# Pairs of delta heads in one inverse, unnormed keys and queries, and smaller first blocks, in a hybrid decoder layer on one core

## The chip, the cores and the metric

The kernel runs on one core of one Trainium2 chip. The metric is device time in microseconds (us). Before the change three runs gave a median of 906.72 us (906.41 to 909.12).

## The reference

One decoder layer is computed in fp32 for a prompt of 512 tokens and for 32 sample tokens (8 sequences of 4), 544 tokens in all, of 1024 features. Cut to what matters:

```python
shift, scale, gate = split(silu(c) @ w_cond + b_cond, 3)
h = x * (1 + scale) + shift
[qa, ka, va, za, qkv_b, zb, a_b, b_b, g_a, g_b] = h @ w_in          # 11280 columns
yA = dilated_window_attention(qa, ka, va) * silu(za)
# branch B, 8 heads of 128, in chunks of the prompt:
q, k, v = silu(causal_conv4(qkv_b))
l2norm = lambda t: t * rsqrt(sum(t * t) + 1e-6)
q = l2norm(q) * 128 ** -0.5;  k = l2norm(k)
lower = strict(beta * (k @ k.T) * decay) + I
u, w = solve(lower, [beta * v, beta * k * exp(cum)])
v_new = u - w @ S
o = (q * exp(cum)) @ S + ((q @ k.T) * decay) @ v_new
S = exp(cum[-1]) * S + (k * tail).T @ v_new
yB = o * rsqrt(mean(o * o) + 1e-6) * b_norm_w * silu(zb)
merged = sigmoid(g_a) * (yA @ w_branch_a) + sigmoid(g_b) * (yB @ w_branch_b)
y = layernorm(ALPHA * x + gate * (merged @ w_out))
```

The caches, the convolution's last rows and the states S are outputs too. The kernel takes the prompt of a head in 4 chunks of 128 tokens.

## The kernel before, in words

**An order made when the program is built.** Nothing that `body` writes runs at once. A recorder notes each operation with its engine, its tiles and a rank (`add`, L271); a list scheduler (`schedule`, L455) with costs of its own then fixes the order of each engine, and one line, L723, sends out every instruction. So all instructions of the profile have line L723, and they are told apart by the names of their tiles. A group noted inside `together` stays in one piece on its engine. Parts of the work are generators with ranks (L2141 to L2204): `delta_rule` has rank 0, `delta_blocks` 1, prompt attention 3; the stream of weights has rank 9 and fills what is left. `threads.set(event, lag)` says how much TensorE work is to pass before another part goes on.

**The stream.** The 11280 columns of `w_in` come as tiles wt of 128 rows x 1024 (one column tile of 128 for all 8 k-tiles). ScalarE rounds a tile to hi, VectorE subtracts for lo (`split`, L867), and TensorE makes three products for each of 8 k-tiles and two halves of the tokens: (hhi,hi), (hlo,hi), (hhi,lo), each 128x272, summed in pp. Raw tiles have three buffers, hi and lo two each.

**The first stage** (L891 to L990). The scale of x comes in four blocks of 256 columns of `w_cond` (`load_cond`, `cond_block`, part 1): each loads wc (2 x 512 KB), xT and W3 for two k-tiles; 8 matmuls of 32x256 in `together`, two small transposes, then x1 = x * scale, split in hi and lo. W3, the columns of the first head's k, q, v, is split too, and each k-tile has 18 products into six sums (pp, pd, pg). Then four blocks of the shift (part 0) follow, which are added to the sums afterwards. TensorE writes these blocks in turn to a pg and the only pb bank (`BANKS`: two pp, two pd, three pg, one pb).

**A delta head** has these steps. `conv_job` (L1205) convolves k, q and v of head h into KQ (two buffers; head h waits until head h-2 has set `freed`) and uv. `delta_blocks(h)` (L1271) makes the decays NTs, transposes KQ through pb, sums the squares of rows (sq) into rc, takes root and reciprocal, transposes rc (pb<-cst,rc), copies it to rrow, writes it to DRAM (dr), reads it back as a broadcast rb, and multiplies KQ by it; so keys and queries are normed. Then NTs becomes beta * decay * k.k and QKd decay * q.k. The 16x16 blocks on the diagonal go through DRAM (dblk) to Ls on 32 partitions, where VectorE inverts them by 15 steps of two operations (tmp, then Tb), in three groups of ten in `together`; Tb goes through DRAM (dtz) to Tc on 128 partitions.

`delta_rule(h)` (L1377) builds the whole inverse XF from Tc in six groups of small matmuls, each in `together`: (Tc,NTs) 32x16, (W,Xc) 32x16, (Tc,NTs) 32x32, (W,XF), then (U,NTs) 64x64 and (XF,U). Then four chunks of state follow (z, vn, S), the norm of the output rows, orow in the single buffer of XF, and its store to dO.

**The end.** `norm_out` (L2296) norms a block of rows after its last product; for the last block of the prompt (tt = 3) the products come in quarters of 256 columns, and VectorE combines each with gp and the residual.

Of the kernel before, what the change touches and what calls it, by code (L numbers as in the profile page):

```python
# [11 lines left out]
F32 = mybir.dt.float32  # L12
# [7 lines left out]
D = 1024  # L20
KT = 8
# [19 lines left out]
S0B = 7  # L41

# [733 lines left out]
def body(ctx, tc, io):  # L776
# [114 lines left out]
    with ExitStack() as fctx:  # L891
# [6 lines left out]
        def load_cond(part, b):  # L898
            pieces[part, b] = fr.tile([128, KT, 256], F32, name="wc", bufs=4)
            for k in (0, 4):  # L900
                sp.dma_start(pieces[part, b][:, k:k + 4], io["w_cb"][part, b, :, k:k + 4])

        for b in range(4):
            load_cond(1, b)
            if not b:
                sp.dma_start(cst, io["const"])
                sp.dma_start(bT, io["bT"])
            sp.dma_start(xT[:, 2 * b:2 * b + 2], io["xT"][:, 2 * b:2 * b + 2])
            sp.dma_start(W3[:, 2 * b:2 * b + 2], io["w3"][:, 2 * b:2 * b + 2])
        for b in range(4):  # L910
            load_cond(0, b)
# [14 lines left out]
        def cond_block(part, b):  # L926

            ps, wc = pb_() if b % 2 else pg(), pieces[part, b]
            rec.rank = -1
            with rec.together():  # L930
                for k in range(KT):
                    q = k % 4
                    pe.matmul(ps[32 * q:32 * q + 32, 0:256], cs[:, k, :], wc[:, k, :], start=(k < 4), stop=(k >= 4),
                              tile_position=(0, 32 * q))
            Y = fr.tile([128, 256], F32, name="Y", bufs=2)
            ve.tensor_copy(Y, ps[:, 0:256])
            pv = ps[:, 256:288].rearrange("p (a b) -> p a b", b=16)
            with rec.together():
                for i in range(2):
                    pe.matmul(pv[:, i, 0:9], Y[:, 128 * i:128 * i + 128], C("selc"), start=True, stop=True)  # L940
            rec.rank = 0
            return pv[:, :, 0:9], bT[:, 8 * part + 2 * b:8 * part + 2 * b + 2, None].to_broadcast([128, 2, 9])
# [3 lines left out]
        for b in range(4):  # L946
            pv, bias = cond_block(1, b)
            kk = slice(2 * b, 2 * b + 2)
            ve.scalar_tensor_tensor(sc[:, kk], pv, 1.0, bias, op0=OP.add, op1=OP.add)
            for k in range(2 * b, 2 * b + 2):  # L950
                se.activation(x1[0][:, k, :SEQ], xT[:, k, :SEQ], AF.Copy, scale=sc[:, k, 0:1])
                if k == 2 * b:
                    ve.tensor_mul(xs[:, kk], xs[:, kk], per_token(sc, 2 * b, 2))
# [4 lines left out]
            hi, lo = (wsp.tile([128, D], F32R, name=n, tag=n)[:, 0:768].rearrange("p (k c) -> p k c", k=2) for n in ("hi", "lo"))  # L958
            se.activation(hi, W3[:, kk, 0:384], AF.Copy)
            ve.tensor_sub(lo, W3[:, kk, 0:384], hi.bitcast(F32))  # L960
            for k in range(2 * b, 2 * b + 2):
                for t in range(3):
                    w, w_ = (x[:, k % 2, 128 * t:128 * t + 128] for x in (hi, lo))
# [18 lines left out]
        for b in range(4):  # L982
            pv, bias = cond_block(0, b)
            kk = slice(2 * b, 2 * b + 2)
            ve.tensor_add(sh[:, kk, 0:9], pv, bias)
# [219 lines left out]
    def conv_job(h, s):  # L1205
# [4 lines left out]
        def begin():  # L1210
            if s == 1:
# [3 lines left out]
                hd.KQ = dl.tile([128, 4, 2, 128], F32, name="KQ")  # L1215
# [47 lines left out]
        if s == 1 and h > 1:  # L1263
            start = (heads[h - 2].freed,)
# [6 lines left out]
    def delta_blocks(h):  # L1271
# [14 lines left out]
        rcf = rc.rearrange("p a c -> p (a c)")  # L1286
        kr = dl.tile([128, 4, 128], F32, name="kr")
        for s in range(2):
# [3 lines left out]
            sq = dl.tile([128, 4, 128], F32, name="sq", bufs=1)  # L1292
            for c in range(4):
                se.activation(sq[:, c], cols128(pt)[:, c], AF.Square, accum_out=rc[:, s, c:c + 1])
            if s == 0:
                rec.either(kr, cols128(pt))
            yield 2.2 + 2 * s
        se.activation(rcf[:, 0:8], rcf[:, 0:8], AF.Sqrt, bias=eps4[:, 0:1])
        ve.reciprocal(rcf[:, 0:8], rcf[:, 0:8])
        ve.tensor_scalar(rc[:, 1], rc[:, 1], qscale, None, op0=OP.mult)  # L1300
# [3 lines left out]
        rec.either(rrow, pn[0:8, 0:128])  # L1304
        dr = dram.tile([8, 128], F32, name=f"dr{h}")
        sp.dma_start(dr, rrow)
        rb = dl.tile([128, 2, 512], F32, name="rb", bufs=1)
        sp.dma_start(rb, dr.rearrange("a b -> (a b)")[None, :].to_broadcast([128, 1024]))
        ve.tensor_mul(rc[:, 2], rc[:, 0], tail[:, h:32:8])
        yield 1.0  # L1310
        QKd = dl.tile([128, 4, 128], F32, name="QKd")
        ve.tensor_mul(KQ.rearrange("p c u i -> p u c i"), KQ.rearrange("p c u i -> p u c i"),
                      rb.rearrange("p u (c i) -> p u c i", i=128))
        for c2 in range(2):
# [8 lines left out]
            for cc in range(2):  # L1323
                c = 2 * c2 + cc
                ve.scalar_tensor_tensor(NTs[:, c, :], pkv[:, cc, 0, :], beta[:, 8 * c + h:8 * c + h + 1], NTs[:, c, :],
                                        op0=OP.mult, op1=OP.mult)
            yield 3.0 if c2 else 14.0
# [4 lines left out]
        diag = lambda t, e: t[:, 16 * e:16 * e + 16, 16 * e:16 * e + 16]  # L1332
        Ls = dl.tile([32, 16, 16], F32, name="Ls", bufs=1)
# [14 lines left out]
        ve.tensor_mul(kr, kr, rc[:, 2, :, None].to_broadcast([128, 4, 128]))  # L1348
# [4 lines left out]
        rec.either(vr, cols128(pt), 0.5)  # L1353

        Tb = dl.tile([32, 16, 16], F32, name="Tb", bufs=1)
        ge.memset(Tb, 0.0)
        tf = Tb.rearrange("p a b -> p (a b)")
        ge.memset(tf[:, 0:256:17], 1.0)
        tmp = dl.tile([32, 64], F32, name="tmp", bufs=1)
        for j0 in range(0, 15, 5):  # L1360
            with rec.together():
                for j in range(j0, j0 + 5):
                    ni, nm = 15 - j, j + 1
                    tv = tmp[:, 0:ni * nm].rearrange("p (a b) -> p a b", b=nm)
                    ve.tensor_mul(tv, Ls[:, j, j + 1:, None].to_broadcast([32, ni, nm]),
                                  Tb[:, j, None, 0:nm].to_broadcast([32, ni, nm]))
                    ve.tensor_sub(Tb[:, j + 1:, 0:nm], Tb[:, j + 1:, 0:nm], tv)
        for e in range(2):
            sp.dma_start(diag(dtz[h], e), Tb[16 * e:16 * e + 16])
        Tc = dl.tile([128, 4, 32], F32, name="Tc")  # L1370
        sp.dma_start(Tc, dtz[h].rearrange("(c b) i m -> (b i) c m", b=4))
        hd.NTs, hd.QKd, hd.kr, hd.vr, hd.rc, hd.Tc = NTs, QKd, kr, vr, rc, Tc
        threads.set(hd.blocks, 0.0)
        threads.set(hd.rule, 36.0)
        yield 0

    def delta_rule(h):  # L1377
        hd = heads[h]
        yield hd.rule
        KQ, NTs, QKd, kr, vr, rc, Tc = hd.KQ, hd.NTs, hd.QKd, hd.kr, hd.vr, hd.rc, hd.Tc  # L1380
        Xc = dl.tile([128, 4, 32], F32, name="Xc", bufs=1)
        ve.transpose(Xc, Tc)
        XF = dl.tile([128, 4, 128], F32, name="XF", bufs=1)
        U = dl.tile([128, 4, 64], F32, name="U", bufs=1)
# [3 lines left out]
        W0 = dl.tile([128, 4, 16], F32, name="W0", bufs=1)  # L1388
        pw = pd()
        pwv = pw[:, 0:64].rearrange("p (s m) -> p s m", m=16)  # L1390
# [8 lines left out]
        pxv = px[:, 0:64].rearrange("p (s m) -> p s m", m=16)  # L1399
        with rec.together():  # L1400
            for c in range(4):
# [10 lines left out]
        W = dl.tile([128, 4, 32], F32, name="W", bufs=1)  # L1412
        pw = pd()
        pwv = pw[:, 0:128].rearrange("p (s m) -> p s m", m=32)
        with rec.together():
            for c in range(4):
                for a in (0, 64):
                    pe.matmul(pwv[a + 32:a + 64, c, :], NTs[a:a + 32, c, a + 32:a + 64], Tc[a:a + 32, c, :],
# [5 lines left out]
        pxv = px[:, 0:128].rearrange("p (s m) -> p s m", m=32)  # L1424
        with rec.together():
            for c in range(4):
# [12 lines left out]
        pwv = pw[:, 0:256].rearrange("p (s m) -> p s m", m=64)  # L1439
        with rec.together():  # L1440
            for c in range(4):
                pe.matmul(pwv[64:128, c, :], NTs[0:64, c, 64:128], U[0:64, c, :],
# [4 lines left out]
        pxv = px[:, 0:256].rearrange("p (s m) -> p s m", m=64)  # L1447
        with rec.together():
            for c in range(4):
# [4 lines left out]

        S = None
        po = pd()
        for c in range(4):
# [12 lines left out]
            rec.either(vn, px[:, 128:256], beta[:, col:col + 1])  # L1470
# [5 lines left out]
            Sn = dl.tile([128, 128], F32, name="S", bufs=3)  # L1476
# [660 lines left out]
    def chain(f, n):  # L2137
        for h in range(n):
            yield from f(h)

    rules = threads.add(chain(delta_rule, 8), 0)  # L2141
    blocks = threads.add(chain(delta_blocks, 8), 1)
# [153 lines left out]
    def norm_out(tt):  # L2296
# [159 lines left out]
```

## Time and profile before

| | |
|---|---|
| median of three runs | 906.72 us (906.41 to 909.12) |
| the profiled execution | 906.21 us |
| its span, first to last instruction | 904.4 us |
| mean granted clock of TensorE | 0.997 |
| TensorE matmuls, busy | 876.3 us, 97% |
| VectorE, busy | 670.3 us, 74% |
| ScalarE, busy | 469.4 us, 52% |
| DMA queue of SyncE and the others, share of 16 engines | 77.5% |

The profile is one execution, in us from the span's start. PE is TensorE's matmul, PEld its loading of weights, DVE VectorE, ACT ScalarE, POOL GpSimd, SP SyncE, which issues the DMAs. `out<-in` are the names of the tiles that an instruction writes and reads. Matmuls overlap in the pipeline, so what one costs the engine is read from start to start, not from its duration. An fp32 matmul is one operation in the code and two instructions in the trace. Behind a "|" stands the idle time before a group, and what ended it; a row such as "PE pp <- DVE lo" gives the total, the count and the longest of one kind of wait.

### The profile page before, as it was taken

The page shows a single profiled execution, that of the slowest core. Times are in us where ns is not written, and L with a number is a line of the kernel's source. Part 1 is how long each engine was busy: PE and PEld are TensorE (multiplying, and loading weights), DVE is VectorE, ACT ScalarE, POOL GpSimd, SP SyncE. Part 2 cuts the span into 40 slices and gives each one's busy share as a digit, 9 for nine tenths or more (in the row PEclk, how much of TensorE's full clock was granted, in tenths as well). Part 3 has the DMA queues.
Part 4 walks back from the last instruction along what each step waited for, and adds up shares of the span by engine and source line. Part 5 has one row for each costly group of instructions (what it writes and reads, how often), then busy time and mean ns, then how long its engine had stood idle before and what let it go on. Part 6 is the DMA issues. An engine that isn't in the chain of part 4 may idle for free.

```text
span 904.4 us, 20926 instructions
## 1 busy us (share of the span) xinstructions
PE 876.3 (97%) x8170; PEld 819.8 (91%) x8170; DVE 670.3 (74%) x1430; ACT 469.4 (52%) x1126; POOL 75.5 (8%) x191
## 2 busy tenths in 40 slices
PE   5999999999999999999999999999999999999995
PEld 3889998888999999998999998899999999989884
DVE  3675545664558989677988896565999799988568
ACT  2456468664578763579754676552442213234331
POOL 0120010010101200011100100011010000001000
PEclk9999999999999999999999999999999999999998
DMA  9766785587868969887878887569779799986943
GB/s 351 307 196 227 226 260 170 201 288 235 251 209 304 300 206 327 267 274 239 252 274 279 282 269 221 186 193 327 294 233 365 249 418 421 376 298 209 358 156 122
DMA packets 107184, 240.09 MB, mean 265 GB/s; under 512 B 30359, under 2 KB 61601, under 8 KB 104397
## 3 DMA queue, kind: packets, MB, share of 16 engines
q1 hardware_dynamic: 107084, 238.76, 77.5%
q8 instruction: 64, 1.05, 0.5%
q14 instruction: 36, 0.29, 0.1%
HBM read 222.40 MB, written 104.00 MB: 361 GB/s over the span
## 4 chain that ended last, share of the span: by engine, by line
PE 86%; DVE 5%; ACT 4%; DMA 3%; issue 1%; SPq 1%; POOL 0%; DVEq 0%; ACTq 0%; POOLq 0%
PE pp L723 64%; PE pg L723 9%; PE pd L723 8%; PE pb L723 4%; DVE acc L723 1%; DMA W<-in_w 1%; DMA dO<-orow 1%; ACT L723 1%; DVE r L723 1%; DMA Ls<-dblk 1%; SPq L723 1%; DVE lo L723 1%; ACT P L723 1%; ACT sq L723 1%; DMA stc<-in_state_conv 0%
## 5 line engine op out<-in xcount | busy, mean ns | idle before, releaser
L723 PE MATMUL pp<-hhi,hi 128*128 128x272 f32 x1360 | 400.3, 294 | 2.3 <-DVE spare L723 1.4
L723 PE MATMUL pp<-hhi,lo 128*128 128x272 f32 x1360 | 400.9, 295 | 1.2 <-DVE lo L723 1.2
L723 PE MATMUL pp<-hlo,hi 128*128 128x272 f32 x1360 | 401.0, 295 | 0.0
L723 PEld LDWEIGHTS pp<-hhi,hi 128*128 128x128 f32 x1360 | 256.4, 188 | 5.7 <-issue 2.0
L723 PEld LDWEIGHTS pp<-hlo,hi 128*128 128x128 f32 x1360 | 256.5, 189 | 4.5 <-issue 3.1
L723 PEld LDWEIGHTS pp<-hhi,lo 128*128 128x128 f32 x1360 | 256.2, 188 | 4.4 <-issue 1.5
L723 ACT ACTIVATE hi<-wt 128x1024 fp32r<-128x1024 f32 (+1 forms) x101 | 103.6, 1026 | 135.9 <-PE pp L723 114.2
L723 DVE TENSOR_TENSOR lo<-wt,hi 128x1024 fp32r<-128x1024 f32 (+1 forms) x101 | 119.0, 1178 | 73.2 <-ACT hi L723 71.8
L723 DVE SCALAR_TENSOR_TENSOR acc<-ext,cw,acc 128x568 f32<-128x568 f32 x72 | 57.5, 798 | 2.0 <-ACT acc L723 1.4
L723 ACT ACT_TABLE_LOAD x38 | 48.8, 1283 | 3.3 <-DVE acc L723 2.0
L723 DVE TENSOR_TENSOR slab<-slab 128x512 f32<-128x512 f32 (+1 forms) x66 | 42.9, 669 | 2.7 <-DMA slab<-in_vs 1.7
L723 DVE TENSOR_REDUCE slab<-slab 128x8 f32<-128x512 f32 (+2 forms) x66 | 42.9, 659 | 0.4
L723 ACT ACTIVATE zt<-pp 128x272 f32<-128x272 f32 x48 | 18.7, 390 | 46.2 <-PE pp L723 44.9
L723 PE MATMUL pp<-ybl,hi 128*128 128x272 f32 x128 | 36.9, 288 | 0.0
L723 PE MATMUL pp<-ybh,lo 128*128 128x272 f32 x128 | 36.8, 288 | 0.0
L723 PE MATMUL pp<-ybh,hi 128*128 128x272 f32 x128 | 36.8, 288 | 0.0
L723 ACT ACTIVATE P<-P,st 128x256 f32<-128x256 f32 (+1 forms) x64 | 31.3, 490 | 9.4 <-DVE st L723 9.2
L723 POOL COPY cx<-ext 128x3 f32<-128x3 f32 (+1 forms) x48 | 23.4, 515 | 100.3 <-ACT ext L723 97.6
L723 DVE CUSTOM_DVE_ANT_0 P<-pg,bias 128x256 f32<-128x256 f32 (+1 forms) x64 | 23.1, 401 | 7.1 <-PE pg L723 6.8
L723 DVE TENSOR_TENSOR tmp<-Ls,Tb 32x15 f32<-32x15 f32 (+7 forms) x120 | 23.2, 193 | 4.9 <-DMA Ls<-dblk 1.6
L723 DVE TENSOR_TENSOR Tb<-Tb,tmp 32x15 f32<-32x15 f32 (+7 forms) x120 | 23.4, 195 | 4.1
L723 ACT ACTIVATE spare<-pp 128x272 f32<-128x272 f32 (+1 forms) x32 | 16.1, 503 | 16.5 <-PE pp L723 16.3
(408 smaller groups left out, 1612.1 us busy)
## 6 DMA issues: line engine op xcount, KB each, us to landing
out_kv_s<-in_cache SPq DMA_DIRECT2D x144, 512.0 KB
wt<-in_w_in SPq DMA_DIRECT2D x85, 512.0 KB
out_kv_s<-in_cache SPq DMA_DIRECT2D x24, 496.0 KB
wc<-in_w_cb SPq DMA_DIRECT2D x16, 512.0 KB
slab<-in_ks SPq DMA_DIRECT2D x32, 256.0 KB
slab<-in_vs SPq DMA_DIRECT2D x32, 256.0 KB
kv<-in_ks SPq DMA_DIRECT2D x16, 512.0 KB
kv<-in_vs SPq DMA_DIRECT2D x16, 512.0 KB
```

The costliest lines, as they stand in the source:

```text
L723: getattr(real[x.engine], x.name)(*map(arg, x.args), **{k: arg(v) for k, v in x.kw.items()})
```

## The change

**Pairs.** Heads 1 and 2, 3 and 4, 5 and 6 are taken together, heads 0 and 7 alone (`TOGETHER`). `decays(h, Ls)`, the first part of the old `delta_blocks`, runs for each head of a pair and puts its blocks into 32 of the 64 partitions of a shared Ls; the substitution runs once for both; Tb goes to dtz by two DMAs a head, and Tc has room for both heads in one buffer. In `delta_rule` the six groups hold the matmuls of both heads; `states(h, XF)` then runs for one head after the other.

```diff
+TOGETHER = ((0,), (1, 2), (3, 4), (5, 6), (7,))
+CHUNKS = ((0, 1), (1, 1), (2, 2), (4, 2), (6, 2))
...
+    def delta_blocks(heads_):
+        n = len(heads_)
+        Ls = dl.tile([32 * n, 16, 16], F32, name="Ls", bufs=1)
+        for i, h in enumerate(heads_):
+            yield from decays(h, Ls[32 * i:32 * i + 32])
+        Tb = dl.tile([32 * n, 16, 16], F32, name="Tb", bufs=1)
...
+        Tc = dl.tile([128, 4 * n, 32], F32, name="Tc", bufs=1)
+        for i, h in enumerate(heads_):
+            for e in range(2):
+                sp.dma_start(diag(dtz[h], e), Tb[32 * i + 16 * e:32 * i + 16 * e + 16])
+        for i, h in enumerate(heads_):
+            sp.dma_start(Tc[:, 4 * i:4 * i + 4], dtz[h].rearrange("(c b) i m -> (b i) c m", b=4))
...
+        threads.set(heads[heads_[-1]].rule, 24.0)
...
-        threads.set(hd.rule, 36.0)
...
+    def delta_rule(heads_):
+        n, last = 4 * len(heads_), heads[heads_[-1]]
...
+        parts = [(4 * i + c, heads[h].NTs[:, c]) for i, h in enumerate(heads_) for c in range(4)]
...
-            for c in range(4):
+            for c, N in parts:
                 for a in range(0, 128, 32):
-                    pe.matmul(pwv[a:a + 32, c, :], NTs[a:a + 32, c, a:a + 32], Tc[a:a + 32, c, 0:16],
+                    pe.matmul(pwv[a:a + 32, c, :], N[a:a + 32, a:a + 32], Tc[a:a + 32, c, 0:16],
```

In TensorE's order, in the stream of weights, the first group of head 1 stands alone before (here a row of matmuls counts operations, two instructions each):

```order
L723 MATMUL pp<-hhi,lo 128x272
L723 MATMUL pp<-hhi,hi 128x272
L723 MATMUL pd<-Tc,NTs 32x16 x16
L723 MATMUL pp<-hlo,hi 128x272
L723 MATMUL pp<-hhi,lo 128x272
```

and now the same group of heads 1 and 2 stands at one place:

```order
L725 MATMUL pp<-hlo,hi 128x272
L725 MATMUL pp<-hhi,lo 128x272
L725 MATMUL pd<-Tc,NTs 32x16 x32
L725 MATMUL pp<-hhi,hi 128x272
L725 MATMUL pp<-hlo,hi 128x272
```

Two groups of 16 have become one of 32; over the whole program the order has as many instructions on TensorE as before.

**Unnormed keys and queries.** KQ is no longer multiplied by the norms. With ss the sum of squares of a row of k, beta / (ss + 4 eps) takes the place of beta (NTs and vn), the root of it scales v, and the sum of squares of q goes into the root that norms the output rows. rrow, dr, rb and the transpose of rc go; kr and vr are scaled by VectorE as they leave PSUM. KQ has three buffers, and head h waits for head h-3.

```diff
-        pn = pb_()
-        pe.transpose(pn[0:8, 0:128], rcf[:, 0:8], ident)
-        rrow = dl.tile([8, 128], F32, name="rrow", bufs=1)
...
-        sp.dma_start(dr, rrow)
...
-        ve.tensor_mul(KQ.rearrange("p c u i -> p u c i"), KQ.rearrange("p c u i -> p u c i"),
-                      rb.rearrange("p u (c i) -> p u c i", i=128))
...
+                ve.tensor_mul(kr, cols128(pt), tail[:, h:32:8, None].to_broadcast([128, 4, 128]))
...
-        rec.either(vr, cols128(pt), 0.5)
+        ve.tensor_mul(vr, cols128(pt), rc[:, 2, :, None].to_broadcast([128, 4, 128]))
...
-        se.activation(rn, rn, AF.Sqrt, bias=eps1[:, 0:1], scale=1.0 / 128)
+        ve.scalar_tensor_tensor(rn, rn, 1.0 / 128, rc[:, 1], op0=OP.mult, op1=OP.add)
+        se.activation(rn, rn, AF.Sqrt)
```

**Shared buffers.** orow takes a buffer of NTs (two), W one of Xc, W0 one of vn; S has two buffers instead of three.

```diff
-        orow = dl.tile([128, 4, 128], F32, name="orow", tag="XF", bufs=1)
+        orow = dl.tile([128, 4, 128], F32, name="orow", tag="NTs")
```

**The first stage.** The scale comes in five blocks (`CHUNKS`, first k-tile and count): the first two have one k-tile each, with half the wc, xT and W3; the shift keeps four blocks of two k-tiles. On the host `w_cond` is laid out in pieces of 128 columns. The first wt, loaded ahead of all, is now loaded behind the shift blocks, as the first of three.

```diff
+        for c, m in CHUNKS:
+            load_cond(1, c, m)
+            if not c:
+                sp.dma_start(bT, io["bT"])
                 sp.dma_start(cst, io["const"])
...
+            sp.dma_start(xT[:, c:c + m], io["xT"][:, c:c + m])
+            sp.dma_start(W3[:, c:c + m], io["w3"][:, c:c + m])
...
-        for i in range(2):
+        for i in range(3):
             raws[i] = wraw.tile([128, D], F32, name="wt", tag="wraw")
```

SyncE's order at the start of the program, before (W is a tile of W3's columns, wc one of `w_cond`'s):

```order
L723 DMA wt<-in_w_in 128x1024
L723 DMA cT<-in_cT 128x72
L723 DMA wc<-in_w_cb 128x1024 x2
L723 DMA cst<-in_const 128x330
L723 DMA bT<-in_bT 128x24
L723 DMA xT<-in_xT 128x1088
L723 DMA W_117<-in_w 128x800
L723 DMA wc<-in_w_cb 128x1024 x2
```

and now:

```order
L725 DMA cT<-in_cT 128x72
L725 DMA wc<-in_w_cb 128x1024
L725 DMA bT<-in_bT 128x24
L725 DMA cst<-in_const 128x330
L725 DMA xT<-in_xT 128x544
L725 DMA W_114<-in_w 128x400
L725 DMA wc<-in_w_cb 128x1024
L725 DMA xT<-in_xT 128x544
L725 DMA W_114<-in_w 128x400
```

wt is gone from the front, and ahead of the first W stand one wc and half an xT. TensorE's order at the start, before:

```order
L723 MATMUL pg<-wc,cs 32x256 x8
L723 MATMUL pg<-cst,Y 128x9 x2
L723 MATMUL pp<-x1h,hi 128x272
L723 MATMUL pd<-x1h,hi 128x272
L723 MATMUL pp<-x1h,hi 128x272
L723 MATMUL pd<-x1h,hi 128x272
L723 MATMUL pg<-x1h,hi 128x272 x2
L723 MATMUL pp<-x1l,hi 128x272
L723 MATMUL pp<-x1h,lo 128x272
L723 MATMUL pp<-x1l,hi 128x272
L723 MATMUL pp<-x1h,lo 128x272
L723 MATMUL pd<-x1l,hi 128x272
```

and now:

```order
L725 MATMUL pg<-wc,cs 32x128 x8
L725 MATMUL pg<-cst,Y 128x9
L725 MATMUL pb<-wc,cs 32x128 x8
L725 MATMUL pp<-x1h,hi 128x272 x2
L725 MATMUL pd<-x1h,hi 128x272 x2
L725 MATMUL pg<-x1h,hi 128x272
L725 MATMUL pp<-x1l,hi 128x272
L725 MATMUL pp<-x1h,lo 128x272
L725 MATMUL pb<-cst,Y 128x9
L725 MATMUL pp<-x1l,hi 128x272
```

The blocks of matmuls with wc are half as wide, and the second one (pb) stands ahead of the first product (pp<-x1h,hi).

**The end.** For the last quarter of the last block the three VectorE operations behind the product and the `bn_aggr` of `norm_out` stand in one `together`.

More of the change, by code (lines that the diff above doesn't have):

```diff
@@ L3 @@
 import re
-from contextlib import ExitStack, contextmanager
+from contextlib import ExitStack, contextmanager, nullcontext
 import numpy as np
@@ L924, in body, with cond_block @@
         ve.tensor_mul(cs[:, :, 0:9], cT, th)
-        def cond_block(part, b):
-            ps, wc = pb_() if b % 2 else pg(), pieces[part, b]
+        def cond_block(part, at, m, other):
+            ps, wc, w = pb_() if other else pg(), pieces[part, at], 128 * m
             rec.rank = -1
@@ L1262, in conv_job @@
         start = ()
-        if s == 1 and h > 1:
-            start = (heads[h - 2].freed,)
+        if s == 1 and h > 2:
+            start = (heads[h - 3].freed,)
         if s == 2 and h:
@@ L1269, in conv_job, with decays @@
         return job
-    def delta_blocks(h):
+    def delta_blocks(heads_):
[4 more added lines that the diff above has]
+        Tb = dl.tile([32 * n, 16, 16], F32, name="Tb", bufs=1)
+        ge.memset(Tb, 0.0)
+        tf = Tb.rearrange("p a b -> p (a b)")
+        ge.memset(tf[:, 0:256:17], 1.0)
+        tmp = dl.tile([32 * n, 64], F32, name="tmp", bufs=1)
+        for j0 in range(0, 15, 5):
+            with rec.together():
+                for j in range(j0, j0 + 5):
+                    ni, nm = 15 - j, j + 1
+                    tv = tmp[:, 0:ni * nm].rearrange("p (a b) -> p a b", b=nm)
+                    ve.tensor_mul(tv, Ls[:, j, j + 1:, None].to_broadcast([32 * n, ni, nm]),
+                                  Tb[:, j, None, 0:nm].to_broadcast([32 * n, ni, nm]))
+                    ve.tensor_sub(Tb[:, j + 1:, 0:nm], Tb[:, j + 1:, 0:nm], tv)
+        Tc = dl.tile([128, 4 * n, 32], F32, name="Tc", bufs=1)
[4 more added lines that the diff above has]
+            sp.dma_start(Tc[:, 4 * i:4 * i + 4], dtz[h].rearrange("(c b) i m -> (b i) c m", b=4))
+            heads[h].Tc = Tc
+        threads.set(heads[heads_[-1]].rule, 24.0)
+        yield 0
+    diag = lambda t, e: t[:, 16 * e:16 * e + 16, 16 * e:16 * e + 16]
+    def decays(h, Ls):
         hd = heads[h]
@@ L1352, in delta_blocks @@
         vr = dl.tile([128, 4, 128], F32, name="vr")
-        rec.either(vr, cols128(pt), 0.5)
[L1355 to L1367, printed above, removed]
@@ L1453, in delta_rule, with states @@
         yield 1.7
+        for i, h in enumerate(heads_):
+            yield from states(h, XF[:, 4 * i:4 * i + 4])
+    def states(h, XF):
+        hd = heads[h]
+        KQ, QKd, kr, vr, rc = hd.KQ, hd.QKd, hd.kr, hd.vr, hd.rc
         S = None
@@ L2135, in body, with chain @@
     of_a = (lambda k: yah[k], lambda k: yal[k])
-    def chain(f, n):
-        for h in range(n):
+    def chain(f):
+        for h in TOGETHER:
             yield from f(h)
-    rules = threads.add(chain(delta_rule, 8), 0)
-    blocks = threads.add(chain(delta_blocks, 8), 1)
+    rules = threads.add(chain(delta_rule), 0)
+    blocks = threads.add(chain(delta_blocks), 1)
     threads.add(gates(), -2)
```

162 lines of the change are left out of this document (74 added, 88 removed).

## Prediction

> **What bounds the kernel now.** I read the page first, then the stages (busy time by stretch), then TensorE's order of time where it is not dense. The page:
>
> ```profile
> span 904.4 us, 20926 instructions
> PE 876.3 (97%) x8170; PEld 819.8 (91%) x8170; DVE 670.3 (74%) x1430; ACT 469.4 (52%) x1126; POOL 75.5 (8%) x191
> ...
> PE 86%; DVE 5%; ACT 4%; DMA 3%; issue 1%; SPq 1%; POOL 0%; DVEq 0%; ACTq 0%; POOLq 0%
> ```
>
> TensorE is busy for 97% of the span and holds 86% of the chain that ended last. The stages (columns: stretch, length, then busy time and instructions of PE, PEld, DVE, ACT, POOL, then PE clock, DMA share, GB/s) say where the rest is:
>
> ```profile
> 0.00:17.00 17.00, 6.09 (x35) 4.01 (x39) 4.13 (x13) 3.76 (x6) 0.51 (x5) 1.00 0.89 327
> 17.00:40.00 23.00, 23.00 (x215) 19.02 (x215) 13.94 (x31) 9.45 (x16) 2.15 (x2) 1.00 0.95 382
> ...
> 500.00:600.00 100.00, 98.61 (x1084) 91.95 (x1083) 75.00 (x203) 64.12 (x171) 6.89 (x19) 1.00 0.73 230
> ```
>
> From 17 us on TensorE always has something; 11 of its 28 idle us lie before 17. So only three things count: time that TensorE spends between products (a busy PE hides it, since matmuls overlap), the start, and the short stalls in which a slow VectorE holds TensorE up. Work saved on VectorE or ScalarE alone counts nothing; VectorE stands at 74%, and TensorE's stream of weight products hides it.
>
> **The shared inverse.** Each head's inverse is six groups of small matmuls between weight products. One group of 32x32 tiles in order of time (start, duration, instruction), then a 64x64 one:
>
> ```profile
> 398.15 0.29 PE L723 MATMUL pp<-hlo,hi 128*128 128x272 f32 x1
> 398.28 0.29 PE L723 MATMUL pp<-hhi,lo 128*128 128x272 f32 x1
> 398.50 0.44 PE L723 MATMUL pd<-Tc,NTs 32*32 32x16 f32 x32
> 398.87 0.40 PE L723 MATMUL pp<-hhi,hi 128*128 128x272 f32 x1
> 399.11 0.29 PE L723 MATMUL pp<-hlo,hi 128*128 128x272 f32 x1
> ...
> 400.71 0.36 PE L723 MATMUL pd<-W,Xc 32*32 32x16 f32 x22
> ```
> ```profile
> 375.33 0.68 PE L723 MATMUL pd<-U,NTs 64*64 64x64 f32 x8
> 375.94 0.40 PE L723 MATMUL pp<-hhi,lo 128*128 128x272 f32 x1
> ```
>
> Undisturbed, the next product starts 0.125 us after the last (398.15 to 398.28). Around the group it is 398.28 to 399.11, 0.83 us for two products (0.25) and the group: 0.58. Of these the matmuls themselves take 0.26: 32 last 0.44, 22 last 0.36, so 8 ns each. The other 0.32 us is paid once a group: 0.09 to enter, 0.11 before the first product can start, 0.11 until the second. A pair pays it once where two heads paid twice. Three pairs, four groups of 32x32 each: 12 x 0.32 = 3.8 us. The 64x64 groups: 0.61 us to the next product, 0.68 for eight less the 0.18 by which the 0.44 above exceeds its 0.26, so 0.50 of work, then 0.11 after and 0.09 before as above: 0.3 fixed, x6 = 1.8. Sum **5.6** (bounds 4.5, if a fifth of the groups stands beside another group and not between products, and 5.8).
>
> Against it, pairs let other small groups stand alone. Counting form changes in the order of TensorE, 226 become 179; pairs (36) and the transposes below (16) would give 52 fewer, so about five come back, 0.16 us each with half a group's cost: **-0.5** (0 to -0.8).
>
> **Unnormed keys and queries.** The transpose of the norms goes, eight times:
>
> ```profile
> 465.05 0.27 PE L723 MATMUL pb<-cst,rc 128*8 128x128 f32 x1
> 465.08 0.38 PE L723 MATMUL pp<-hlo,hi 128*128 128x272 f32 x1
> 465.29 0.29 PE L723 MATMUL pp<-hhi,lo 128*128 128x272 f32 x1
> ```
>
> 465.05 to 465.29 is 0.24 for it and a product of 0.125: 0.11 each, x8 = 0.9; I take **0.8**, since two stand beside other work. What else goes, off the path: the round trip of the norms through DRAM with its broadcast, the multiplication of KQ, half of the norm's small steps. What comes: kr and vr are scaled from PSUM on VectorE. All of it lies beside products; if that cover were gone, VectorE would still be lighter by more than it takes on, because of the next rows.
>
> **VectorE's substitution** runs five times for eight, on 64 partitions for a pair:
>
> ```profile
> L723 DVE TENSOR_TENSOR tmp<-Ls,Tb 32x15 f32<-32x15 f32 (+7 forms) x120 | 23.2, 193 | 4.9 <-DMA Ls<-dblk 1.6
> L723 DVE TENSOR_TENSOR Tb<-Tb,tmp 32x15 f32<-32x15 f32 (+7 forms) x120 | 23.4, 195 | 4.1
> ```
>
> Three of eight go: 3/8 x 46.6 = 17.5 us of VectorE, if 64 partitions take as long as 32 (an estimate, since the elements in a row of the tile stay the same). This is worth only the stalls that it causes, since ten operations stand together and what comes behind them waits:
>
> ```profile
> 566.41 0.16 DVE L723 TENSOR_TENSOR Tb<-Tb,tmp 32x15 f32<-32x15 f32 x1
> 566.62 0.44 DVE L723 SCALAR_TENSOR_TENSOR spare<-spare,pp 128x272 f32<-128x272 f32 x1
> ```
> ```profile
> PE pp L723 <- DVE spare L723: 1.4, 1, 1.4
> ...
> PE pp L723 <- DVE lo L723: 1.2, 1, 1.2
> ```
>
> Both waits of TensorE end behind such ten (the second also behind the landing of Ls): 2.6 us for eight substitutions; three fewer give **1.0** (from -2, if pairs stall it anew, to 2.6, if both go). Late next is then only the weights' own split.
>
> **The start.** TensorE, in order of time, and what ScalarE waited for:
>
> ```profile
> 8.59 2.27 PE L723 MATMUL pg<-wc,cs 128*32 128x256 f32 x16 [8.59 <-DMA wc<-in_w_cb]
> ...
> 14.10 0.59 PE L723 MATMUL pp<-x1h,hi 128*128 128x272 f32 x1 [1.67 <-ACT x1h L723]
> 14.49 0.43 PE L723 MATMUL pd<-x1h,hi 128*128 128x272 f32 x1
> ...
> 16.89 1.65 PE L723 MATMUL pb<-wc,cs 128*32 128x256 f32 x16
> ...
> 18.70 0.28 PE L723 MATMUL pd<-x1l,hi 128*128 128x272 f32 x1
> ```
> ```profile
> 12.59 0.84 ACT L723 ACTIVATE hi<-W 128x768 fp32r<-128x768 f32 x1 [7.74 <-DMA W<-in_w]
> ```
> ```profile
> 0.74 0.39 SPq L723 DMA_DIRECT2D wt<-in_w_in  x1
> ```
> ```profile
> wc<-in_w_cb SPq DMA_DIRECT2D x16, 512.0 KB
> ```
> ```profile
> xT<-in_xT SPq DMA_DIRECT2D x4, 544.0 KB
> ...
> W<-in_w SPq DMA_DIRECT2D x4, 400.0 KB
> ```
>
> The first product waits for W, landed at 12.57. Ahead of it stand wt (512 KB), two wc, xT, W and three small tables, 2.76 MB. Now wt goes behind, and wc, xT and W are half: 512 + 512 + 272 + 200 KB less, 1.53 MB, which at the 382 GB/s of the second stretch is 4.0 us: W at 8.6. A second way: what is left, 1.23 MB, is little more than what had landed at 8.59 when TensorE could begin (wt and the first of the two wc, 1.05 MB): 9.0. I take 8.7. But in the new order of TensorE the second block's matmuls stand ahead of the first product; their 512 KB come next, 1.4 us later, so TensorE goes on at about 10.1 and is then fed: 1.0 MB for each k-tile take 2.7 us, its 18 products 2.3 warm (18 x 0.125) and 4.1 cold (18 x 0.227, from 14.49). So the dense part starts 14.1 - 10.1 = 4.0 earlier, but holds one half-wide block more. A full one, warm:
>
> ```profile
> 27.40 1.07 PE L723 MATMUL pb<-wc,cs 128*32 128x256 f32 x16
> ...
> 28.63 0.29 PE L723 MATMUL pd<-x1h,lo 128*128 128x272 f32 x1
> ```
>
> 1.1 us without its product, and some 0.5 for the small transposes behind it; half of the matmuls and all of the entering and leaving is about 1.2. Left: **2.8**. Bounds: 4.0, if that block costs nothing; 0.5, if W shares the queues with the second block (1.3 us) and the last shift block, whose data come no earlier than now, is waited for (1.0).
>
> The Trainium skill's DMA: Bandwidth & Descriptors (section Bandwidth) speaks against the halving: it asks for 1 MiB a transfer for 75% of peak, and measured 32% at 64 KB. By a rate between, 55% of its 435 GB/s, an estimate from that page, W would land near 10.5 and the second block near 12.7, and the start would be worth 0.2. The trace does not agree for transfers that are in flight together: pieces of 400 to 544 KB moved at 382 GB/s.
>
> **The end**, a reordering behind the last product:
>
> ```profile
> 894.66 0.41 DVE L723 SCALAR_TENSOR_TENSOR r<-pp,gp 128x256 f32<-128x256 f32 x1
> ...
> 899.14 2.06 DVE L723 SCALAR_TENSOR_TENSOR r<-r,mv,lnb 128x512 f32<-128x512 f32 x3
> ```
>
> VectorE runs without a gap from 894.66 to 901.2; the same operations stand there in another order, and as large a store is last: 0 (±0.3).
>
> **Sum.** 5.6 - 0.5 + 0.8 + 1.0 + 2.8 = 9.7 us against the profiled execution's 906.21 (span 904.4 and 1.8 around it). The median of the runs, 906.72, lies 0.5 above it; I take the sum off the median: **897.0**. With all upper bounds 5.8 + 0.9 + 2.6 + 4.0 = 13.3, so 893.4; with all lower ones 4.5 + 0.5 - 0.8 - 2 + 0.5 = 2.7, so 904.0.
>
> **Rivals.** (a) *The start gives nothing*: transfers, not TensorE, set when the first stage ends. For: DMA share 0.95 there. Against: TensorE without a gap from 14.1 on. 906.7 - 6.9 = 899.8. (b) *The half clock lasts*: TensorE at the start is now fed in bursts. A product took 0.227 us at 14.49 and 0.125 from 18.70 on; if all 72 products of the first four k-tiles ran at 0.227 and not only 15, 57 x 0.10 = 5.8 us would go: 902.8. Against: cold products (4.1 us a k-tile) are slower than their data (2.7), so TensorE gets no pause. The Trainium skill's TensorE: Matmul & The Clock Gate (Part 1) puts the half clock down to idle windows of some 3.4 us; by that rule the wait between the first block and the second keeps the clock low once more, but not what follows. (c) *Pairs make their own waits*: a pair is longer on VectorE and ScalarE between the groups, and its products in between are as few as before; eight of the 9.7 us go to new stalls: 905. (d) *Slower*: the output rows now share the two buffers of NTs. A store of them takes
>
> ```profile
> 399.78 6.14 DMA dO<-orow
> ```
>
> and with a pair, output rows of both heads and NTs of the next two pass through two buffers. If the next NTs reach VectorE sooner than 6.14 us after the store's issue, VectorE stands, with the split of the weights (lo) behind it. The split runs one tile ahead, 48 x 0.125 = 6.0 us, which covers one such wait and not two in a row: 6.1 us a pair, three pairs 18.4: 915.4. Against: VectorE's order has one or two weight splits, 6 to 12 us, between a head's output rows and the NTs that follow. (e) *More*: every bound is met at its better end: 893.4. That pairs are not formed is excluded: the order shows groups of twice the matmuls.
>
> **Numbers.** Forecast 0.62, (a) 0.14, (b) 0.05, (c) 0.09, (d) 0.06, (e) 0.04. Within 0.3%, about what a measurement of this kernel can tell from no change, is 904.0 to 909.4: only (c). Faster: forecast, (a), (b), (e): 0.85; same 0.09; slower 0.06. The range runs from 893.0 to 902.8: it holds forecast, (a), (b) and (e), 0.85 in all.
>
> **What would show it.** Right: a pair's group of 32x32 takes 0.58 + 0.26 = 0.84 us out of the products; no transposes of rc; first product near 11 us, with TensorE dense from 10 on and the last product of the sums some 3 us earlier; TensorE's waits for spare and lo below 2 us. Wrong: products at 0.227 us past 16 us (b), gaps in TensorE between 10 and 40 us (a), TensorE waiting for vn, W, XF or lo inside pairs (c), VectorE idle before NTs with a store of dO as its releaser (d).

## The result, and the profile after

The changed kernel took 900.25 us (median of 4 runs, 899.23 to 902.66) against 906.71 us: a ratio of 0.9931, 95% interval 0.9915 to 0.9947. That is faster, as forecast, inside the range, and 3.25 us short of the 897.0 forecast. The profiled execution was the slowest of the four, 902.66 us; the difference of the two profiled executions is 906.21 - 902.66 = 3.55 us, and the accounts below are of these two.

The page after:

```profile
span 900.9 us, 20727 instructions
PE 873.6 (97%) x8178; PEld 822.2 (91%) x8178; DVE 650.8 (72%) x1341; ACT 449.9 (50%) x1076; POOL 74.1 (8%) x173
...
PE 83%; DVE 7%; ACT 4%; DMA 4%; issue 1%; SPq 1%; DVEq 0%; ACTq 0%
```

VectorE and ScalarE have lost 20 us each, and TensorE is still busy for 97% of the span; by the prediction this loss counts for nothing, and no run tests it alone. The stages of the start, with the columns of the prediction's table (busy time of PE, PEld, DVE, ACT, POOL, clock, DMA share, GB/s), and TensorE's and ScalarE's rows there:

```profile
0.00:17.00 17.00, 9.60 (x82) 7.93 (x83) 5.29 (x19) 5.12 (x9) 0.52 (x5) 1.00 0.88 324
17.00:40.00 23.00, 22.71 (x216) 18.83 (x215) 14.51 (x34) 10.45 (x21) 1.77 (x2) 1.00 0.96 384
```
```profile
7.68 0.52 ACT L725 ACTIVATE hi<-W 128x384 fp32r<-128x384 f32 x1 [4.86 <-DMA W<-in_w]
```
```profile
9.08 1.08 PE L725 MATMUL pb<-wc,cs 128*32 128x128 f32 x16 [1.84 <-DMA wc<-in_w_cb]
10.09 0.82 PE L725 MATMUL pp<-x1h,hi 128*128 128x272 f32 x2
...
13.63 0.35 PE L725 MATMUL pg<-x1l,hi 128*128 128x272 f32 x1
13.82 0.29 PE L725 MATMUL pg<-x1h,lo 128*128 128x272 f32 x1
```

W has landed by 7.68 us instead of 12.59, the second block starts at 9.08, and products run from 10.09 on, at half speed (one every 0.22 us) only to 13.6. The spacing of the products shows this; the clock column, with 1.00 for the whole stretch, does not. A pair's group of 32x32, with the product ahead of it and two behind:

```profile
224.74 0.29 PE L725 MATMUL pp<-hhi,lo 128*128 128x272 f32 x1
224.96 0.73 PE L725 MATMUL pd<-Tc,NTs 32*32 32x16 f32 x64
225.61 0.39 PE L725 MATMUL pp<-hhi,hi 128*128 128x272 f32 x1
225.85 0.28 PE L725 MATMUL pp<-hlo,hi 128*128 128x272 f32 x1
```

224.74 to 225.85 is 1.11 us, less two products 0.86: two heads in one group, where 0.58 was paid for one. So far all is as forecast. What is not as forecast is the list of TensorE's longest waits behind the start (total, times, longest), here of the changed kernel:

```profile
PE pp L725 <- ACT yah L725: 2.1, 1, 2.1
...
PE pd L725 <- ACT U L725: 1.4, 1, 1.4
PE pp L725 <- DVE zt L725: 1.3, 3, 0.5
PE pb L725 <- DMA S<-in_state_delta: 1.2, 2, 0.7
PE pg L725 <- DMA rbo<-dO: 1.0, 1, 1.0
```

The waits for spare (1.4) and lo (1.2) are gone, as forecast; yah and U stand in their place, and behind each of the two TensorE was granted half its clock for 3.41 us:

```profile
242.44:245.85 3.41, 3.41 (x18) 3.41 (x17) 1.88 (x3) 1.16 (x3) 0.00 (x0) 0.50 1.10 443
809.05:812.46 3.41, 3.41 (x15) 3.30 (x16) 1.45 (x2) 1.18 (x2) 0.00 (x0) 0.50 0.36 154
```

To count this, take the stream of weights from its first product with hhi or hlo to its last. Its row (length, then PE busy) before, and after:

```profile
43.97:841.91 797.94, 791.04 (x7559) 749.80 (x7558) 606.00 (x1305) 437.35 (x1074) 71.50 (x183) 1.00 0.79 266
```
```profile
40.53:837.97 797.44, 788.60 (x7551) 751.28 (x7550) 587.05 (x1214) 417.89 (x1022) 71.39 (x165) 1.00 0.78 261
```

Length less busy time is idle time: 6.90 us before, 8.84 after. A stretch of 3.41 us at half clock does the work of 1.7, so it costs 1.7; before had none in the stream, after two, 3.4. Busy time less that is the **work**: 791.0 us before, 785.2 after. Idle time and half clock together are called **losses** below: 6.9 before, 12.2 after. The stream starts 3.44 us earlier, its work is 5.85 us less, its losses 5.35 us more, and what lies behind it (62.5 and 62.9 us) 0.4 more: 3.54, the 3.55 measured. Each of these figures is of one execution, and they scatter. In the kernels below that have the same work in the stream and little half clock, work comes out between 783.7 us (the first stage as before) and 787.3 (less slack). The stream begins between 39.39 and 41.47 us in all traces with small first blocks, and between 42.92 and 43.97 in the three with the old first stage.

### The profile page after: what moved, and what is told of

The parts are those of the page before. It is cut to its first block, busy times and chain, and to the rows that moved or that the text cites. A ratio compares the mean times of both kernels' runs of the same rounds, so it can differ in the third digit from the quotient of the medians.

```text
span 900.9 us, 20727 instructions
## 1 busy us (share of the span) xinstructions
PE 873.6 (97%) x8178; PEld 822.2 (91%) x8178; DVE 650.8 (72%) x1341; ACT 449.9 (50%) x1076; POOL 74.1 (8%) x173
## 4 chain that ended last, share of the span: by engine, by line
PE 83%; DVE 7%; ACT 4%; DMA 4%; issue 1%; SPq 1%; DVEq 0%; ACTq 0%
PE pp L725 63%; PE pg L725 9%; PE pd L725 7%; PE pb L725 4%; DVE slab L725 1%; ACT L725 1%; DMA S<-in_state_delta 1%; DVE lo L725 1%; DMA rbo<-dO 1%; DVE acc L725 1%; DVE r L725 1%; DMA slab<-in_bias_s 1%; SPq L725 1%; DMA out_kv_s<-in_cache 1%; DMA wc<-in_w_cb 1%
## 5 line engine op out<-in xcount | busy, mean ns | idle before, releaser
L725 ACT ACTIVATE zt<-pp 128x272 f32<-128x272 f32 x48 | 18.8, 391 | 40.6 <-PE pp L725 38.4
L725 ACT ACTIVATE P<-P,st 128x256 f32<-128x256 f32 (+1 forms) x64 | 31.3, 493 | 12.7 <-DVE st L725 12.6
L725 PEld LDWEIGHTS pp<-ybh,hi 128*128 128x128 f32 x128 | 24.2, 189 | 0.1
L725 PEld LDWEIGHTS pp<-ybl,hi 128*128 128x128 f32 x128 | 24.1, 188 | 0.1
```

The source lines that it names most:

```text
L725: getattr(real[x.engine], x.name)(*map(arg, x.args), **{k: arg(v) for k, v in x.kw.items()})
```

## The experiments

The theory: start and shared groups gave what was forecast, and new waits with half clock behind them took back half of it. The first rival: only the start gave anything. Each kernel below is the changed one with one edit, if nothing else is said. Its ratio is to the kernel before.

**All heads alone.**

```diff
-TOGETHER = ((0,), (1, 2), (3, 4), (5, 6), (7,))
+TOGETHER = tuple((h,) for h in range(8))
```

> All heads alone again, everything else of the change kept. Theory (a group of both heads saves its entering and leaving on TensorE's path: 12 x 0.30 + 6 x 0.35 us by the changed kernel's trace, less 0.5 for groups that stand alone now): 5.2 us slower than the changed kernel's 900.25 us, 905.4 us; 902.3 if the stall of 1.44 us before the pair's last group, with the half clock behind it (1.7 us), goes with the pairs. Rival (the whole gain is the start, and what pairs save is lost to groups that stand alone): 900.3 us, within 1 us.

Measured 910.76 us, ratio 1.0038 (1.0026 to 1.0051): slower than before the change. Its stream, and TensorE's longest waits in it:

```profile
40.35:846.33 805.98, 792.38 (x7552) 751.39 (x7551) 606.55 (x1323) 428.91 (x1051) 67.52 (x183) 1.00 0.78 260
```
```profile
PE pp L725 <- DVE zt L725: 3.8, 4, 1.8
PE pb L725 <- DVE KQ L725: 2.0, 1, 2.0
PE pb L725 <- DVE vns L725: 1.7, 1, 1.7
PE pp L725 <- ACT yah L725: 1.6, 1, 1.6
PE pg L725 <- DVE o L725: 1.5, 1, 1.5
```

With one stretch of half clock its work is 792.4 - 1.7 = 790.7 us: the pairs are worth 5.5 us of work, between 3.4 and 7.0 by the scatter of that figure, which settles the first rival. The other 5 us come from losses of 15.3 instead of 12.2 and from the choice of profiled executions. So in this order the other parts of the change make a slower kernel, by waits: against before the stream starts 3.6 us earlier, its work is about the same (790.7 and 791.0), and its losses are 8.4 us more.

**The first stage as before.**

```diff
-CHUNKS = ((0, 1), (1, 1), (2, 2), (4, 2), (6, 2))
+CHUNKS = ((0, 2), (2, 2), (4, 2), (6, 2))
...
-        for i in range(3):
+        for i in range(2):
             raws[i] = wraw.tile([128, D], F32, name="wt", tag="wraw")
```

> The first stage as before (four scale blocks of two k-tiles, the first weight tile loaded ahead of all), the rest of the change kept. Theory (3.4 us of the gain are the start, and nothing later gives them back): 903.7 us, the first product of the weight stream at 44.0 us as before instead of 40.5. Rival (the samples' attention on VectorE sets when the first product with yah can start, and TensorE's time saved ahead of it is waited away there): 900.3 us, with a shorter wait before yah.

Measured 902.44 us, ratio 0.9957 (0.9940 to 0.9974), the stream from 43.90 us on. The wait before yah was the same 2.09 us, so the rival's shorter wait isn't there. Of the 3.4 us 2.2 show in the medians; the losses of this order are 9.2 and its work 783.7. The interval overlaps that of the changed kernel, so it is the stream's beginning that shows the start's gain, and not this time.

**Only the first weight tile ahead again** (the second hunk alone).

> Only the place of the first weight tile undone (512 KB, loaded ahead of all again), the small blocks kept. Theory (the start is bound by what lands ahead of the first block): 512 KB at the 382 GB/s of the second stretch are 1.3 us, so 901.6 us and the weight stream from 41.9 us on. Rival (the small blocks alone make the gain, and other transfers fill the gap): 900.3 us.

Measured 901.69 us, ratio 0.9946 (0.9929 to 0.9962). The stream began at 41.16 us, 0.6 later than the changed kernel's and not 1.4. That lies inside the scatter of the other kernels with small first blocks (39.39 to 41.47), and the times are not clear of each other: a price of that tile is not shown, and that 901.6 us was hit is luck. The blocks are the larger part of the start, by these executions 43.90 - 41.16 = 2.7 of 3.4 us.

**The bias tiles negated on GpSimd.** TensorE waited for U, which stood on ScalarE behind a bias tile:

```profile
239.21 0.50 ACT L725 ACTIVATE slab<-slab 128x352 f32<-128x352 f32 x1 [2.50 <-DMA slab<-in_bias_s]
239.73 0.59 ACT L725 ACTIVATE U<-pd 64x512 f32<-64x512 f32 x1
```
```profile
238.65 0.29 PE L725 MATMUL pp<-hlo,hi 128*128 128x272 f32 x1
240.37 1.14 PE L725 MATMUL pd<-XF,U 64*64 64x64 f32 x16 [1.44 <-ACT U L725]
```

```diff
-            se.activation(sb[x], sb[x], AF.Copy, scale=-1.0)
+            ge.tensor_scalar(sb[x], sb[x], -1.0, None, op0=OP.mult)
```

> The samples' biases are negated on GpSimd instead of ScalarE, so that ScalarE no longer stands behind the landing of a bias tile with the eviction of U queued behind it. Theory (the 1.44 us wait of TensorE for U at 238.65 us, with the stretch of half clock behind it, 3.41 us long and so 1.7 us dear, belongs to this order and comes in most executions): 3.1 us faster, 897.1 us, no half clock near 242 us. Rival (the stall is a chance of the one profiled execution): 900.3 us, within 1 us.

Measured 902.72 us, ratio 0.9947 (0.9927 to 0.9968). The wait for U was gone, and the half clock near 242 us; the order behind it is another, and has waits of its own:

```profile
PE pp L725 <- DVE zt L725: 3.2, 5, 1.7
...
PE pp L725 <- DVE spare L725: 1.5, 1, 1.5
PE pg L725 <- ACT P L725: 1.3, 2, 1.1
```

Theory and rival both miss it: the losses are 12.7 again, and the time is not clear of the changed kernel's. The last experiment shows something beside its own question: with the same order of TensorE and ScalarE at that place ScalarE waited 0.97 us for the bias and TensorE not at all. So the order alone does not bring the wait for U; it depends on when the bias lands in an execution. The other three runs of the changed kernel are 1.7 to 3.4 us faster than the profiled one, which fits, but whether they had the wait is not known.

**More slack in the order.** The scheduler leaves more time between a result and its use on another engine:

```diff
-        return 0.1 if p.transfer is None else 1.0
+        return 0.4 if p.transfer is None else 1.0
```

> The changed kernel, ordered by a scheduler that leaves 0.4 us instead of 0.1 us between a result and another engine's use of it; the work is the same. Theory (TensorE's work has fallen by the 5.85 us that were forecast, and what is missing is 12.2 us of idle time and half clock inside the weight stream where the order is too tight; before had 6.9): such losses fall to about 7, 895.5 us, with the work without them at 785.2 us as now. Rival (the waits come from transfers and from whole chains on VectorE, which slack in the order does not mend): 900.3 us, within 1 us.

Measured 925.66 us, ratio 1.0215 (1.0196 to 1.0233).

```profile
40.63:863.85 823.22, 797.34 (x7552) 758.30 (x7551) 589.07 (x1220) 422.08 (x1021) 66.02 (x165) 0.98 0.77 257
```
```profile
PE pp L725 <- DVE zt L725: 4.8, 3, 3.3
PE pg L725 <- DVE o L725: 4.3, 1, 4.3
PE pb L725 <- DVE NTs L725: 3.9, 2, 2.9
PE pd L725 <- DMA Tc<-dtz: 2.8, 1, 2.8
```

Theory and rival both fall: idle time is 25.9 us and half clock costs 18.8. Most of these waits are for a chain's last step (o, Tc, zt). A reading that fits, and that was not tested apart, is that slack added to each step of a long chain makes the chain late where TensorE meets it.

**More slack behind transfers** (1.0 to 2.5 us in the same line).

> The changed kernel, ordered with 2.5 us instead of 1.0 us allowed behind the landing of a transfer; the work is the same. Theory of the tight order: half of the waits end behind landings or behind an engine held by one, so losses in the weight stream fall from 12.2 to about 9, 897 us. Rival (landings only seem to be the releasers, and the losses move elsewhere): 900.3 us, within 1.5 us.

Measured 913.69 us, ratio 1.0086 (1.0072 to 1.0100), with 15.7 us idle and 5.1 of half clock. Theory and rival fall here too; the longest waits are for zt (5.3 us in three).

**Four pairs.**

```diff
-TOGETHER = ((0,), (1, 2), (3, 4), (5, 6), (7,))
+TOGETHER = ((0, 1), (2, 3), (4, 5), (6, 7))
```

> Heads 0+1, 2+3, 4+5, 6+7 in pairs, so four pairs instead of three. Theory (each pair saves 4 x 0.30 + 2 x 0.35 = 1.9 us of TensorE's path): work in the weight stream 783.3 us instead of 785.2, and 898.4 us if the losses stay. Rival (the losses decide: pairing the first head delays its inverse and the start of the states, and a pair's longer evictions stall TensorE): 901 us or more with the work at 783.3 us all the same.

Measured 904.41 us, ratio 0.9983 (0.9972 to 0.9993).

```profile
40.48:841.18 800.70, 788.46 (x7551) 750.41 (x7550) 582.33 (x1178) 418.00 (x1015) 71.90 (x159) 1.00 0.78 261
```

Two stretches of half clock leave a work of 785.0 us, where the changed kernel has 785.2 and 783.3 was expected: no saving of the fourth pair is seen, though the scatter of that figure could hide 1.9 us. The losses are 15.7; the rival's time came, its work did not. Of the twelve groups that heads 0 and 7 have in the changed kernel's trace only two stand between weight products; the others stand beside small groups of attention, with which they share entering or leaving. So the price of 0.3 us a group, which was read between products, was not theirs to save.

**The new first stage alone, in the kernel before.** The edit is the change's first stage with its load order, and nothing else of it.

```diff
+        for c, m in CHUNKS:
+            load_cond(1, c, m)
...
+        for i in range(3):
             raws[i] = wraw.tile([128, D], F32, name="wt", tag="wraw")
```

> The kernel before with nothing but the new first stage (small first blocks and the first weight tile behind them). Theory (the start's 3.4 us are kept to the end): 903.4 us against 906.8, the weight stream from 40.5 us on, its work at 791.0 us as before. Rival (they are waited away later, at the end of the samples' attention on VectorE): 906.8 us, within 1 us.

Measured 902.85 us, ratio 0.9966 (0.9954 to 0.9979): 3.6 us by the medians, as the theory has it.

```profile
40.68:839.03 798.35, 791.97 (x7560) 751.44 (x7558) 609.99 (x1309) 432.93 (x1070) 75.83 (x183) 1.00 0.80 267
```

In the profiled executions the stream starts 3.3 us earlier. With one stretch of half clock its work is 790.3 us, 0.8 less than before's though no work in the stream was changed: that is noise. This kernel too waits 2.09 us before yah, which before did not, with half clock behind it. So the rival's wait did come; but the waits for spare and lo of the kernel before are gone from this order, and its losses, 8.1, are only 1.2 above before's.

**The late samples' attention with less VectorE.** The wait before yah, at about 804 us in most of these kernels, is where the stream runs out of products that don't need the samples' attention. First guess: VectorE is too slow for it.

```diff
-                                    lambda: s2.tile([128, D], F32, name="kv", tag="cache"), 1024, 2.0, (ve,), late_over)
+                                    lambda: s2.tile([128, D], F32, name="kv", tag="cache"), 1024, 2.0, (ve, ve, ve, ge), late_over)
```

> The changed kernel with every fourth multiplication of the late samples' attention (8 of 32, 1.22 us each on VectorE) on GpSimd. Theory (where the stream of weights meets the end of that attention, at 804 us, VectorE's chain is the bound, so TensorE's saved time is waited away there: 2.09 us idle and a stretch of half clock worth 1.7): the chain ends earlier by up to 9.8 us of VectorE, TensorE's wait before yah falls below 0.5 us, 896.5 us. Rival (the wait is the order's chance, and another takes its place): 900.3 us, within 1 us. Second rival (GpSimd holds VectorE up, or its slower multiplications become the chain): 902 us or more, VectorE's own rows longer than 1.22 us.

> The same eighth to GpSimd in the kernel before, as a control. Theory (before the change TensorE reached that place 6 us later and waited for nothing there but 0.4 us): 906.5 us, within 1 us, so the move pays only behind the change. Rival (VectorE's relief is worth as much in any kernel, because less of VectorE's work stands in the way of the weights' split): 903.5 us or less.

Measured, in the changed kernel 902.91 us, ratio 0.9965 (0.9951 to 0.9979), and in the kernel before 908.95 us, ratio 1.0023 (1.0013 to 1.0033). Both are slower for it by 2 to 3 us. The profiled execution of the first was the fastest of its eight, 899.98 us. In it TensorE waits twice at the same place, right after each other:

```profile
PE pp L725 <- ACT yah L725: 1.6, 1, 1.6
PE pg L725 <- DVE o L725: 1.5, 1, 1.5
```

and VectorE, from 682 to 806 us, has the longer waits, in the changed kernel and in this one:

```profile
DVE lo L725 <- ACT hi L725: 6.4, 5, 3.2
```
```profile
DVE lo L725 <- ACT hi L725: 11.3, 7, 4.4
```

The theory falls: with 8 multiplications less VectorE waits longer in its fixed order, behind ScalarE's half of the weights' split, and the joint is no better (1.49 and 1.61 us). That VectorE's load does not end the chain is not shown by it, since GpSimd's slower multiplications came into the same chain. The second rival's time came. Its sign came in part: GpSimd took twice as long for one, and single multiplications of VectorE took up to 2.7 us, while their median stayed at 1.21 (the later half of them, in the kernel before: count, then the shortest, median and longest in ns):

```profile
L723 DVE TENSOR_TENSOR kv<-kv,Sb x12: 1206/1211/2715, 761.5 to 801.7; 128x1024 f32<-128x1024 f32 x12
L723 POOL TENSOR_TENSOR kv<-kv,Sb x4: 2398/2881/4123, 762.5 to 793.8; 128x1024 f32<-128x1024 f32 x4
```

**Less slack** (0.1 to 0.02 us in the scheduler's line).

> The changed kernel, ordered with 0.02 us instead of 0.1 us between a result and another engine's use of it; the work is the same. After 0.4 us gave 925.7 us with 44.7 us of idle time and half clock, theory (slack delays the chains of heads and samples, and TensorE then waits for them at the joints, so less slack shortens them): losses in the weight stream below 12.2 us, 898 us. Rival (0.1 us is about the true distance, and a tighter order makes TensorE stand behind operands that are not there): 903 us or more, with many small waits.

Measured 900.21 us, ratio 0.9933 (0.9921 to 0.9945): as the changed kernel.

```profile
39.95:835.96 796.01, 787.30 (x7556) 749.23 (x7554) 588.96 (x1221) 417.53 (x1017) 66.14 (x165) 1.00 0.78 260
```

The losses are 8.7 us, with no half clock, as the theory has it; but this order has 787.3 us of work, 2.1 more than the changed kernel's, which takes back more than half of that.

**Eight buffers instead of seven for the late cache tiles.** In the changed kernel nothing stands between the attention's last matmul and yah; before, 15 products stood there, and TensorE did not wait (first and last row):

```profile
808.71 0.27 PE L723 MATMUL pg<-cst,o 128*128 128x128 f32 x1
...
810.69 0.30 PE L723 MATMUL pp<-yah,hi 128*128 128x272 f32 x1
```

```profile
804.36 0.27 PE L725 MATMUL pg<-cst,o 128*128 128x128 f32 x1
806.73 0.52 PE L725 MATMUL pp<-yah,hi 128*128 128x272 f32 x2 [2.09 <-ACT yah L725]
```

The chain between them (os, ya on VectorE, yah on ScalarE) takes 2.37 us, about 19 products; in other kernels it took as little as 1.9. The traces so far, by the products that the order left there:

| kernel | products between | TensorE idle before yah | half clock at this place |
|---|---|---|---|
| before, less slack | 15 | 0 | no |
| bias on GpSimd | 13 | 0 | no |
| first weight tile ahead | 10 | 0.36 us | no |
| four pairs | 6 | 1.42 us | yes |
| all heads alone, more slack (both kinds), an eighth on GpSimd (both) | 0 | 1.6 us, with 1.5 to 4.3 for o just ahead | yes |
| the changed kernel, old first stage, new first stage alone | 0 | 2.09 us | yes |

```diff
-S0B = 7
+S0B = 8
```

> The changed kernel with eight instead of seven buffers for the cache tiles of the late samples' attention; TensorE's order is the same up to about 660 us, and behind it 41 products of the weight stream stand between that attention's last matmul and the first product with yah, where there were none. Theory (at that joint the loss of 2.09 us and of 1.7 us in half clock comes from the order alone: the chain from the last matmul to yah took 2.37 us, about 19 products, and the attention's tiles come late because they wait for buffers): no wait before yah over 0.4 us, no half clock there, 3.8 us less, 896.5 us. Rival (in most executions the wait was not there, or it moves to another place): 900.3 us, within 1 us.

Measured 895.92 us (894.75 to 897.21), ratio 0.9891 (0.9869 to 0.9912). This beats both kernels. The stream, and the joint:

```profile
39.39:829.40 790.01, 784.55 (x7551) 747.97 (x7550) 586.90 (x1214) 417.40 (x1022) 70.36 (x165) 1.00 0.78 263
```
```profile
795.57 0.27 PE L725 MATMUL pg<-cst,o 128*128 128x128 f32 x1
800.83 0.29 PE L725 MATMUL pp<-yah,hi 128*128 128x272 f32 x1
```

41 products fill the 5.26 us, there is no half clock in the stream, and the losses are 5.5 us, less than before the change. The step from the changed kernel is 4.3 us by the medians where 3.8 were expected. In the profiled executions the stream is 7.4 us shorter: 3.8 of it are the joint, and 3.1 the wait for U with its half clock, which this execution did not have. And ScalarE at the place of the former wait for U, in the same order as in the changed kernel:

```profile
236.47 0.50 ACT L725 ACTIVATE slab<-slab 128x352 f32<-128x352 f32 x1 [0.97 <-DMA slab<-in_bias_s]
236.99 0.59 ACT L725 ACTIVATE U<-pd 64x512 f32<-64x512 f32 x1
```

## Why the prediction was right, and the step of it that failed

- **What bounds the kernel**: right as far as it goes. TensorE's work fell by what was forecast for TensorE, and 20 us less on VectorE and as much on ScalarE left the losses no smaller; no run tests that part alone.
- **The start**: 2.8 forecast, 3.44 in the trace, 3.3 in the trace of the new first stage alone, with a scatter of about 1 us either way. The steps hold (W by 7.7, forecast 8.7; the second block at 9.08, forecast 10.1). By the rate that was worked out from the Trainium skill's DMA: Bandwidth & Descriptors (section Bandwidth) W would have landed near 10.5; the trace does not agree for transfers of 200 to 512 KB that are in flight together.
- **Shared groups, other switches and transposes**: 5.6 - 0.5 + 0.8 = 5.9 forecast, 5.85 in the stream's work, 5.5 for the pairs alone. So close a match is partly luck, since the work of one order differs from another's by up to 3.6 us; and five form changes at 0.16 us make 0.8, where the forecast took 0.5. A group of 32x32 of a pair costs 0.86 us (forecast 0.84).
- **The step that failed is the stalls**, the term of 1.0 us with its sentence that only the weights' own split is late next. The two waits that it named went. But it counted only waits that the substitution ends, and the change deals out the whole order anew: in its order stood a wait of 2.09 us before yah with half clock behind it, 3.8 us, in no part of the code that was touched. In the two profiled executions the term is -5.35 and not +1.0, of which 3.1 (U and its half clock) did not come in the other traced execution of the same order at that place. With the joint mended, the stream's losses are 1.4 us below before's, and the time, 895.92 us, is near where the sum had put it (897.0); but that is a kernel with one more buffer than the one that was forecast.
- **The rivals**: by its time alone, 900.25 us, (a) with its 899.8 would have fitted better than the forecast; the traces exclude it. None of the others was it either. The first stage kept its gain (a), the half clock ended at 13.6 us (b), none of the two longest waits is a pair's own (c: in the profiled execution U is a pair's, but a bias tile's landing held it), and VectorE never waited for a store of output rows ahead of NTs (d). A rival that the prediction lacked: TensorE reaches the joint where it needs another chain's end before the order has products left.
- **Open**: why the kernel without pairs has 15.3 us of losses was not taken apart further. Its longest waits end behind zt, KQ and vns.

## What to carry to other kernels

Where the order of the engines is made ahead by a scheduler, price a change in two sums: the work that it takes off the busiest engine, which came out near the forecast here, and the waits, which are dealt out anew everywhere and were most of the error (6.4 us in the profiled executions, against 0.6 at the start). Look then for the joints, the places where the filler runs out before a side chain has ended, and count the products that the order leaves there against the length of the chain's end. Here one buffer more, with which the order put the side chain's end ahead of 41 products, gained 4.3 us, and moving a part of the chain to a slower engine lost 2 to 3.

## What the runs showed of the hardware that was not expected

- A wait of 1.44 us ahead of a group of small matmuls, and one of 2.09 us, were each followed by 3.41 us at half clock, so each cost about twice its length. The length of a wait does not decide it: the kernel before waited 1.39 us (for spare) without half clock, and the kernel with all heads alone 1.99 us (for KQ) and 1.77 us (for zt).
- In the changed kernel the two stretches of half clock start 809.05 - 242.44 = 566.61 us apart, 166 times 3.413 us; with four pairs 812.32 - 617.76 = 194.56, 57 times. So half clock begins on a grid of 3.41 us. Cut into windows on this grid, the streams of the fourteen traces have twelve windows at full clock in which TensorE idled for 2.03 us or more, and half clock followed each; it followed none with less than 1.35 us. Between, both occur: 1.35 us from 239.03 us in the changed kernel was followed, 1.77 us from 618.32 us with all heads alone was not. What decides there was not settled.
- The Trainium skill's TensorE: Matmul & The Clock Gate (Part 1) has the half clock come after at least one idle window of some 3.4 us. The length of the stretch agrees with that window, but here a window that was idle for less than half was enough.
- 64 partitions took VectorE nearly as long as 32 in the substitution: by trace, 195.8 and 199.2 ns a step (tmp, then Tb) for the pairs, against 193.1 and 195.0 before.
